# Both halves of the split activations in one 512-column matmul, one PSUM bank per output tile, and modulation pieces on TensorE in pairs

## The chip, the cores and the metric

The kernel runs on one core of a Trainium2 chip. TensorE multiplies, VectorE (DVE) and ScalarE (ACT) do the elementwise work, the queue of SyncE (SP) issues the weight transfers from HBM. The metric is the device time of one execution in microseconds: the median of three runs was 2352.77 us (2349.78 to 2356.88).

## The reference, cut to what matters

Two decoder layers over 256 tokens of width 2048. Each has a mixer and a SwiGLU feed-forward block of inner width 5632, each followed by a residual, a layer norm, and a modulation by vectors computed from the conditioning vector `c`:

```
for layer in range(2):
    mod = silu(c) @ w_ada[layer] + b_ada[layer]              # 6 vectors of 2048
    sh1, sc1, g1, sh2, sc2, g2 = split(mod, 6)
    h = x * (1 + sc1) + sh1
    y = even_mixer(h) if layer == 0 else odd_mixer(h)        # attention + S5 | sliding-window attention
    x = layer_norm(ALPHA * x + g1 * y)
    h = x * (1 + sc2) + sh2
    y = (silu(h @ w_gate) * (h @ w_up)) @ w_down
    x = layer_norm(ALPHA * x + g2 * y)
```

All is float32. Batch is one, so every weight is read from HBM once, for 256 tokens.

## The kernel before

**Layout and arithmetic.** Activations lie transposed: 128 features on the partitions, the 256 tokens along the free dimension, 16 such tiles for a width of 2048. TensorE takes float32r operands. To keep float32 accuracy every operand is split into a high part and the remainder. A weight tile becomes `wh` (a cast on ACT, L262) and `wl` (a subtraction on DVE, L263); an activation tile becomes `hh` and `hl` (in other stages `ah`/`al`, `oh`/`ol`, `ch`/`cl`, `fah`/`fal`). A product of a 128x128 weight tile and a 128x256 activation tile is three matmuls into the same 256 columns of PSUM, wh·hi, wh·lo and wl·hi (L1236 to L1238). This text calls the three a trio. High parts and low parts lie in separate tiles of SBUF.

**Units, pieces, groups.** The weights come as pieces of 512 KB (128x1024): eight weight tiles, one unit. The units are read in the order that `_plan` writes out: phases, each a list of groups, each a list of (k, output tile) pairs. `_k_outer` takes all output tiles of the group for one k before the next k, `_o_outer` finishes one output tile before the next. The phases that matter here: `k2`, `v`, `q`, `glu`, `o0` (mixer of layer 0, about 163 to 516 us), `g00`, `d00`, `g01`, `d01` (its feed-forward block, in two halves of the inner width, to 1286 us), `c1`, `cv`, `c2`, `o1` (mixer of layer 1, to 1566 us), and `g10` to `d11`. A g phase computes gate and up tiles for 22 inner tiles f, a d phase multiplies these by w_down for 16 output tiles.

Pieces wait in a ring of six (`RING`); a piece's slot is given back when its split is done, and then SP issues the next piece. The split tiles `wh`/`wl` have three buffers (`NSPLIT`), so the split of a unit waits until TensorE has done with the unit three before it.

**Modes and PSUM.** Four banks of PSUM (512 float32 columns each) hold sums of the stream, four others serve everything else. In mode B two output tiles share a bank, each in 256 columns. In mode A (phases `v`, `cv`) activations are the stationary operand and 512 columns of weights the moving one (L1259). When a group is done, `evac_group` empties its banks: in a g phase silu on ACT (L1193), product on DVE (L1194), cast on ACT (L1196), remainder on DVE (L1197). In `o0`, `o1` and the d phases `evac_slot` adds a finished tile into the residual z with one DVE instruction (`z_evac`, L924), followed by the statistics of the layer norm.

**Modulation pieces.** Between the weights lie pieces of `w_ada`. Most are multiplied by `c` and summed on DVE (`ada_rows`, L535). Those of five blocks in layer 0 go to TensorE (`ada_block`, L557, `ADA_PE`): a piece holds two k tiles of 512 columns, each multiplied by a stationary operand of 32 columns, in a quarter of the array (`tile_position`); four k tiles in a row use the four quarters. Eight pieces make a block, 40 pieces in all.

**What sets the order.** Code is emitted in the order of the stream loop at the end of `build`. A scheduler then orders each engine's instructions by a simulated time line, keeping the order of instructions that carry the same stamp (`c.front`: splits, loads, sums of modulation pieces). Each engine executes its list strictly in that order.

Of the kernel before, what the change touches and what calls it, by code (L numbers as in the profile page):

```python
# [17 lines left out]
T = 256  # L18
# [38 lines left out]
def _plan():  # L57
    """Phases after the first one: lists of groups (kind, array, tiles of (k, out column tile))."""
# [6 lines left out]
    ph.append(("o0", [("oab", _k_outer(ks, [4 * g + i for i in range(4)])) for g in range(3)]  # L65
               + [("oab", _o_outer(ks, [12, 13, 14, 15]))]))
    for layer in range(2):
        gu, dn = f"gu{layer}", f"dn{layer}"
        if layer == 1:
            ph.append(("c1", [("c", _k_outer(ks, [16, 17, 0, 1, 2, 3, 4, 5]))]))  # L70
            ph.append(("cv", [("c", _k_outer(ks, [18, 19]))]))
            ph.append(("c2", [("c", _k_outer(ks, [6, 7, 8, 9])), ("c", _k_outer(ks, [10, 11, 12, 13])),
                              ("c", _k_outer(ks, [14, 15]))]))
            ph.append(("o1", [("oc", _k_outer(ks, list(range(8)))), ("oc", _k_outer(ks, [8, 9, 10, 11])),
                              ("oc", _o_outer(ks, [12, 13, 14, 15]))]))
        for half in range(2):
            f0 = 22 * half
            sizes = [4] + [2] * 9 if half == 0 else [2] * 11
# [12 lines left out]
def _ada_plan(ph):  # L91
    """Where the pieces of each modulation vector are read: phases -> list of (layer, vector)."""
# [12 lines left out]
def _ada_pieces(l, v):  # L105
    """Pieces of a modulation vector: (l, v, out tile, half of k), or (l, v, block of 4 out tiles, pair of k tiles, 1)."""
# [3 lines left out]
    pcs = [p for _, _, p in sorted([((i + 0.5) / len(a), 0, p) for i, p in enumerate(a)]  # L110
# [20 lines left out]
class Group:  # L131
    def __init__(self, ctx, phase, gi, tiles, mode, nslots, wide=False):
# [9 lines left out]
        self.wide = wide  # L142
# [9 lines left out]
class Ctx:  # L152
# [114 lines left out]
def build(tc, I, out):  # L267
# [3 lines left out]
    with ExitStack() as es:  # L271
        c = Ctx(tc, I, out, es)

# [96 lines left out]
        def s5_params():  # L370
# [51 lines left out]
            # q = (lambda_bar - 1) / lambda  # L422
# [35 lines left out]
            # chunk tables of the rotation  # L458
# [11 lines left out]
            # powers of the output matrices  # L470
# [13 lines left out]
            # powers of the input matrices, turned to stationary operands  # L484
# [37 lines left out]
        accs = {}  # L522

        def ada_front(info, t):
            if len(info) == 4:
                ada_rows(info, t)
            else:
                ada_block(info, t)
# [14 lines left out]
        def ada_block(info, t):  # L543
# [15 lines left out]
            if kg == 7:  # L559
# [27 lines left out]
        hh = [c.slot(0, F32R, "hh"), c.slot(1, F32R, "hh")]  # L587
        hl = [c.slot(2, F32R, "hl"), c.slot(3, F32R, "hl")]

        def hsel(pair, t):  # L590
            return pair[t // 8][:, 256 * (t % 8):256 * (t % 8) + 256]
# [32 lines left out]
        for k in range(KT):  # L624
# [16 lines left out]
            A.copy(hsel(hh, k), xt)  # L641
            V.tensor_sub(hsel(hl, k), xt, hsel(hh, k).bitcast(F32))
            h_hi, h_lo = hsel(hh, k), hsel(hl, k)
            for hf in range(2):
# [3 lines left out]
                for i in range(n_st // 2):  # L648
# [4 lines left out]
                    PE.matmul(o, lhsT=wh[:, W], rhs=h_hi, start=(k == 0 and s % 2 == 0), stop=False, skip_group_check=True)  # L653
                    PE.matmul(o, lhsT=wh[:, W], rhs=h_lo, start=False, stop=False, skip_group_check=True)  # L654
                    PE.matmul(o, lhsT=wl[:, W], rhs=h_hi, start=False, stop=(k == KT - 1), skip_group_check=True)
# [36 lines left out]
        def s5_run(hf):  # L692
# [64 lines left out]
            if hf:  # L757
                S["sh"], S["sl"] = c.slot(9, F32R, "sh"), c.slot(8, F32R, "sl")

            def parts(q):  # L760
                W = slice(512 * q, 512 * q + 512)
                A.copy(S["sh"][:, W], S["s"][:, W])
                V.tensor_sub(S["sl"][:, W], S["s"][:, W], S["sh"][:, W].bitcast(F32))
# [97 lines left out]
        def fox(hd):  # L861
# [39 lines left out]
            W = slice(256 * hd, 256 * hd + 256)  # L901
            A.copy(S["ah"][:, W], op[:, 0:256])
            V.tensor_sub(S["al"][:, W], op[:, 0:256], S["ah"][:, W].bitcast(F32))
            c.aux_put(i3)

# [100 lines left out]
        def ln_tile(L, t, hi, lo):  # L1006
# [600 lines left out]
```

## Time and profile before

| | |
|---|---|
| median of three runs | 2352.77 us |
| profiled execution, first to last instruction | 2353.8 us (the page gives no other time of it) |
| TensorE matmul busy | 2294.5 us, 97% |
| TensorE weight load busy | 2181.5 us, 93% |
| VectorE busy | 1633.4 us, 69% |
| ScalarE busy | 1089.5 us, 46% |
| DMA | 581.66 MB, 247 GB/s on average |
| mean granted TensorE clock | 0.988 |

The profile marks a matmul as busy from its start until its last result is written. Neighbouring matmuls overlap in that, so a busy share near 100% doesn't say how fast they follow each other. That is read from the distances between their starts, in the timeline, or from the number of matmuls in a window.

### The profile page before, as it was taken

The numbers are of one execution on the slowest core, as the hardware profiler recorded it, in microseconds if no ns is written. First come the engines' busy times: TensorE is split into PE (matmuls) and PEld (weight loads), VectorE is DVE, ScalarE is ACT, GpSimd is POOL, SyncE is SP. The second block draws the span as 40 slices with busy tenths as digits, with TensorE's granted clock in tenths as the row PEclk, the third lists the DMA queues.
The fourth block names the chain that finished last, engine by engine and source line by source line (L and its number), as shares of the span: only waits on it lengthen the run. The fifth ranks groups of instructions, "written<-read, shape, count | busy, mean of one in ns | idle before, by whom it ended". The sixth has DMA issues, their size and how long they took to land.

```text
span 2353.8 us, 46216 instructions
## 1 busy us (share of the span) xinstructions
PE 2294.5 (97%) x18990; PEld 2181.5 (93%) x18990; DVE 1633.4 (69%) x2818; ACT 1089.5 (46%) x1657; POOL 5.1 (0%) x11
## 2 busy tenths in 40 slices
PE   7999999999999999999999999999999999999997
PEld 5787787789999999999999988999999999999996
DVE  7638866878777777777786988787666444444466
ACT  3455464356444333444444765565443333444344
POOL 0000000000000000000000000000000000000000
PEclk8999999999999999999999999999999999999998
DMA  8998767858988899898875766357777665666652
GB/s 316 339 324 305 260 223 287 301 186 275 310 311 312 309 302 316 312 311 309 309 254 161 259 232 208 117 154 251 261 266 240 182 186 181 184 183 183 185 181 97
DMA packets 161123, 581.66 MB, mean 247 GB/s; under 512 B 18080, under 2 KB 18608, under 8 KB 160528
## 3 DMA queue, kind: packets, MB, share of 16 engines
q1 hardware_dynamic: 159984, 575.49, 72.9%
q8 instruction: 148, 2.42, 0.4%
q10 hardware_dynamic: 720, 2.66, 0.3%
q0 software_dynamic: 208, 0.57, 0.1%
q14 instruction: 63, 0.52, 0.1%
HBM read 576.55 MB, written 2.10 MB: 246 GB/s over the span
## 4 chain that ended last, share of the span: by engine, by line
PE 92%; DVE 3%; DMA 2%; ACT 2%; issue 1%; ACTq 0%; SPq 0%; DVEq 0%; POOLq 0%
PE acc L1236 27%; PE acc L1238 27%; PE acc L1237 27%; PE acc L1259 1%; PE aux L557 1%; PE ab L630 1%; DMA w<-in_ada_s 1%; DMA w<-in_w_ab 1%; DVE wl L263 1%; ACT wh L262 1%; PE aux L1091 0%; PE aux L787 0%; PE aux L1118 0%; ACT u L703 0%; PE acc L654 0%
## 5 line engine op out<-in xcount | busy, mean ns | idle before, releaser
L263 DVE TENSOR_TENSOR wl<-w,wh 128x1024 fp32r<-128x1024 f32 (+1 forms) x712 | 863.0, 1212 | 606.0 <-ACT wh L262 603.1
L262 ACT CAST wh<-w 128x1024 fp32r<-128x1024 f32 (+1 forms) x712 | 738.7, 1038 | 1025.1 <-PE acc L1237 785.1
L1236 PE MATMUL acc<-hh,wh 128*128 128x256 f32 x3296 | 932.1, 286 | 14.8 <-ACT hh L1017 13.2
L1237 PE MATMUL acc<-hl,wh 128*128 128x256 f32 x3296 | 932.6, 285 | 0.0
L1238 PE MATMUL acc<-hh,wl 128*128 128x256 f32 x3296 | 919.4, 285 | 0.8 <-DVE wl L263 0.8
L1236 PEld LDWEIGHTS acc<-hh,wh 128*128 128x128 f32 x3296 | 634.6, 193 | 25.5 <-ACT hh L1017 14.4
L1237 PEld LDWEIGHTS acc<-hl,wh 128*128 128x128 f32 x3296 | 636.2, 193 | 1.2 <-issue 1.0
L1238 PEld LDWEIGHTS acc<-hh,wl 128*128 128x128 f32 x3296 | 628.0, 193 | 6.5 <-issue 4.5
L1237 PE MATMUL acc<-fal,wh 128*128 128x256 f32 x1408 | 398.3, 283 | 0.0
L1236 PE MATMUL acc<-fah,wh 128*128 128x256 f32 x1408 | 398.1, 283 | 0.0
L1238 PE MATMUL acc<-fah,wl 128*128 128x256 f32 x1408 | 397.5, 283 | 0.0
L535 DVE CUSTOM_DVE_ANT_0 w<-w,crow 128x1024 f32<-128x1024 f32 x280 | 340.9, 1219 | 1.1 <-DMA w<-in_ada 1.0
L1236 PEld LDWEIGHTS acc<-fah,wh 128*128 128x128 f32 x1408 | 270.3, 192 | 0.0
L1237 PEld LDWEIGHTS acc<-fal,wh 128*128 128x128 f32 x1408 | 270.3, 192 | 0.0
L1238 PEld LDWEIGHTS acc<-fah,wl 128*128 128x128 f32 x1408 | 269.7, 192 | 0.1
L1236 PE MATMUL acc<-ch,wh 128*128 128x256 f32 x256 | 73.8, 290 | 0.0
L1238 PE MATMUL acc<-ch,wl 128*128 128x256 f32 x256 | 73.3, 288 | 0.4 <-DVE wl L263 0.4
L1237 PE MATMUL acc<-cl,wh 128*128 128x256 f32 x256 | 73.6, 288 | 0.0
L1193 ACT ACTIVATE ftmp<-acc 128x256 f32<-128x256 f32 x88 | 33.5, 383 | 49.3 <-PE acc L1238 49.3
L924 DVE SCALAR_TENSOR_TENSOR z<-acc,mod,z 128x256 f32<-128x256 f32 x96 | 41.1, 478 | 14.3 <-PE acc L1238 14.3
L1237 PEld LDWEIGHTS acc<-cl,wh 128*128 128x128 f32 x256 | 48.9, 191 | 1.9 <-issue 1.8
L1236 PEld LDWEIGHTS acc<-ch,wh 128*128 128x128 f32 x256 | 48.8, 191 | 1.5 <-issue 1.3
(335 smaller groups left out, 2270.0 us busy)
## 6 DMA issues: line engine op xcount, KB each, us to landing
w<-in_w_gu SPq DMA_DIRECT2D x352, 512.0 KB, 4.5
w<-in_ada SPq DMA_DIRECT2D x320, 512.0 KB, 4.6
w<-in_w_dn SPq DMA_DIRECT2D x176, 512.0 KB, 4.4
w<-in_ada_s SPq DMA_DIRECT2D x64, 512.0 KB, 6.1
w<-in_w_ab SPq DMA_DIRECT2D x40, 512.0 KB, 5.1
w<-in_w_c SPq DMA_DIRECT2D x40, 512.0 KB, 4.3
w<-in_w_oab SPq DMA_DIRECT2D x32, 512.0 KB, 5.5
w<-in_w_oc SPq DMA_DIRECT2D x32, 512.0 KB, 4.0
```

Of the source, the lines that this page charges most:

```text
L262: self.front(nc.scalar.copy(wh[:, :n], src), "act")
L263: self.front(nc.vector.tensor_sub(wl[:, :n], src, wh[:, :n].bitcast(F32)))
L535: c.front(V.tensor_tensor_reduce(t, t, crow[:, 1024 * half:1024 * half + 1024], scale=1.0, scalar=0.0, op0=ALU.mult, op1=ALU.add, accum_ou ...
L557: PE.matmul(bank[32 * j:32 * j + 32, :], lhsT=cs[:, k:k + 32], rhs=t[:, 512 * i:512 * i + 512], start=(k < 4), stop=(k >= 12), skip_group_ ...
L630: PE.matmul(abank[32 * j:32 * j + 32, 0:256], lhsT=cs[:, kk:kk + 32], rhs=t[:, 256 * j:256 * j + 256], start=(q == 0), stop=(q == 3), skip ...
L924: ins = V.scalar_tensor_tensor(zt(L, t), ps_, L["g"][:, t:t + 1], zt(L, t), op0=ALU.mult, op1=ALU.add)
L1193: A.activation(sg, b[:, 0:256], AF.Silu)
L1236: PE.matmul(dst, lhsT=wh[:, W], rhs=hi, start=first, stop=False, skip_group_check=True)
L1237: PE.matmul(dst, lhsT=wh[:, W], rhs=lo, start=False, stop=False, skip_group_check=True)
L1238: PE.matmul(dst, lhsT=wl[:, W], rhs=hi, start=False, stop=(g.left[o] == 0), skip_group_check=True)
L1259: PE.matmul(dst, lhsT=act[:, X], rhs=ww[:, c0:c0 + w], start=first, stop=(last and act is lo), skip_group_check=True)
```

## The change

Activation tiles are laid out in pairs: high and low part of one tile side by side, 512 columns (`pair_of`, `hi_of`, `lo_of`, `both_of`). A new mode D is used for all d phases, for `o0` and `o1` behind their first group, and for all groups of a g phase behind its first one, which now have one f each instead of two. In it a trio is two matmuls (`mm2`): wh with 512 columns, hi and lo at once, into a whole bank, and wl with the 256 columns of hi into the bank's right half. An output tile thus has a bank of its own, and whoever empties it adds the two halves. Phases in mode D other than g take their tiles by `_o_outer`. The modulation pieces of TensorE come two at a time.

```diff
-    ph.append(("o0", [("oab", _k_outer(ks, [4 * g + i for i in range(4)])) for g in range(3)]
-               + [("oab", _o_outer(ks, [12, 13, 14, 15]))]))
+    ph.append(("o0", [("oab", _k_outer(ks, [0, 1, 2, 3]))]
+               + [("oab", _o_outer(ks, [4 * g + i for i in range(4)])) for g in range(1, 4)]))
...
-            sizes = [4] + [2] * 9 if half == 0 else [2] * 11
+            sizes = [4] + [1] * 18 if half == 0 else [1] * 22
...
-            gs = [(dn, _k_outer(kk, [4 * g + i for i in range(4)])) for g in range(3)]
-            gs.append((dn, (_o_outer if half else _k_outer)(kk, [12, 13, 14, 15])))
-            ph.append((f"d{layer}{half}", gs))
+            ph.append((f"d{layer}{half}", [(dn, _o_outer(kk, [4 * g + i for i in range(4)])) for g in range(4)]))
...
-            for i in range(2):
-                k = 2 * kg + i
-                j = k % 4
-                PE.matmul(bank[32 * j:32 * j + 32, :], lhsT=cs[:, k:k + 32], rhs=t[:, 512 * i:512 * i + 512], start=(k < 4),
-                          stop=(k >= 12), skip_group_check=True, tile_position=(0, 32 * j))
+            for j in range(4):
+                k = 2 * kg + j
+                PE.matmul(bank[32 * j:32 * j + 32, :], lhsT=cs[:, k:k + 32], rhs=(t, t2)[j // 2][:, 512 * (j % 2):512 * (j % 2) + 512],
+                          start=(kg == 0), stop=(kg == 6), skip_group_check=True, tile_position=(0, 32 * j))
...
+        def both_of(P, t):
+            return P[t // 4][:, 512 * (t % 4):512 * (t % 4) + 512]
...
+        def mm2(bank, wh, wl, P, k, first, last):
+            PE.matmul(bank, lhsT=wh, rhs=both_of(P, k), start=first, stop=False, skip_group_check=True)
+            PE.matmul(bank[:, 256:512], lhsT=wl, rhs=hi_of(P, k), start=False, stop=last, skip_group_check=True)
...
         def z_evac(L, t, ps_, stats=True):
-            ins = V.scalar_tensor_tensor(zt(L, t), ps_, L["g"][:, t:t + 1], zt(L, t), op0=ALU.mult, op1=ALU.add)
-            if t == KT - 1:
-                c.front(ins)
+            for src in ps_:
+                ins = V.scalar_tensor_tensor(zt(L, t), src, L["g"][:, t:t + 1], zt(L, t), op0=ALU.mult, op1=ALU.add)
+                if t == KT - 1:
+                    c.front(ins)
...
+                    if g.mode == "D":
+                        bg_, bu = g.banks[0], g.banks[1]
+                        A.copy(gs, bg_[:, 256:512])
+                        V.tensor_tensor(gs, bg_[:, 0:256], gs, ALU.add)
+                        A.copy(us, bu[:, 256:512])
+                        V.tensor_tensor(us, bu[:, 0:256], us, ALU.add)
+                        A.activation(sg, gs, AF.Silu)
+                        V.tensor_tensor(a, sg, us, ALU.mult)
```

On TensorE, at the turn from the first g phase to the first d phase, the rows before are plain trios; a d group has two output tiles in one bank (`acc_8478`), one trio of each, then two in the next bank:

```order
L1236 MATMUL acc_8212<-hh_5427,wh_8363 128x256
L1237 MATMUL acc_8212<-hl_5429,wh_8363 128x256
L1238 MATMUL acc_8212<-hh_5427,wl_8364 128x256
L1236 MATMUL acc_8478<-fah_5448,wh_8393 128x256
L1237 MATMUL acc_8478<-fal_5451,wh_8393 128x256
L1238 MATMUL acc_8478<-fah_5448,wl_8394 128x256
L1236 MATMUL acc_8478<-fah_5448,wh_8393 128x256
L1237 MATMUL acc_8478<-fal_5451,wh_8393 128x256
L1238 MATMUL acc_8478<-fah_5448,wl_8394 128x256
L1236 MATMUL acc_8485<-fah_5448,wh_8393 128x256
```

In the changed kernel the trio is the pair L608 and L609. The rows here are those at the end of the fifth unit (`wh_7858`) of that d phase and the start of the sixth (`wh_7884`); `hp_5277` holds the last two activation tiles that the g phase made, `wh_7810` belongs to the third unit:

```order
L608 MATMUL acc_7876<-hp_5276,wh_7858 128x512
L608 MATMUL acc_7816<-hp_5277,wh_7810 128x512
L609 MATMUL acc_7816<-hp_5277,wl_7811 128x256
L609 MATMUL acc_7876<-hp_5276,wl_7859 128x256
L608 MATMUL acc_7876<-hp_5276,wh_7858 128x512
L609 MATMUL acc_7876<-hp_5276,wl_7859 128x256
L608 MATMUL acc_7876<-hp_5276,wh_7884 128x512
L608 MATMUL acc_7947<-hp_5272,wh_7884 128x512
L609 MATMUL acc_7876<-hp_5276,wl_7885 128x256
```

The last trio of the first output tile (`acc_7816`, k = 21) stands two units behind the rest of its unit, and the buffer of the third unit is held until then.

On DVE, in the first g phase, one group of two f stands like this before (`wl` rows are splits, ISA rows are sums of a modulation piece):

```order
L1194 TENSOR_TENSOR ftmp_5447<-ftmp_5447,acc_7132 128x256
L263 TENSOR_TENSOR wl_7390<-w_7293,wh_7389 128x1024
L1194 TENSOR_TENSOR ftmp_5447<-ftmp_5447,acc_7139 128x256
L1197 TENSOR_TENSOR fal_5452<-ftmp_5447,fah_5449 128x256
L263 TENSOR_TENSOR wl_7430<-w_7321,wh_7429 128x1024
L535 ISA w_7327,adap_7319<-w_7327,crow_100 128x1024
L535 ISA adap_7319 128x1
L1197 TENSOR_TENSOR fal_5452<-ftmp_5447,fah_5449 128x256
```

After, a group has one f, and these are its rows:

```order
L1214 TENSOR_TENSOR ftmp_5271<-acc_7490,ftmp_5271 128x256
L262 TENSOR_TENSOR wl_7584<-w_7509,wh_7583 128x1024
L534 ISA w_7515,adap_6889<-w_7515,crow_100 128x1024
L534 ISA adap_6889 128x1
L1216 TENSOR_TENSOR ftmp_5271<-acc_7493,ftmp_5271 128x256
L262 TENSOR_TENSOR wl_7619<-w_7534,wh_7618 128x1024
L534 ISA w_7540,adap_6889<-w_7540,crow_100 128x1024
L534 ISA adap_6889 128x1
L1218 TENSOR_TENSOR ftmp_5271<-ftmp_5271 128x256
L262 TENSOR_TENSOR wl_7644<-w_7559,wh_7643 128x1024
L1225 TENSOR_TENSOR hp_5276<-ftmp_5271,hp_5276 128x256
```

Four evacuation instructions for two f became four for one f, with splits and sums between them.

On TensorE the two halves of a pair of modulation pieces stand next to each other in some places (here in `o0`):

```order
L609 MATMUL acc_4814<-hp_4149,wl_4779 128x256
L556 MATMUL aux_4562<-w_4748,cs_97 32x512 x2
L556 MATMUL aux_4562<-w_4754,cs_97 32x512 x2
L609 MATMUL acc_4882<-hp_3406,wl_4804 128x256
L608 MATMUL acc_4882<-hp_3406,wh_4803 128x512
```

In others (here in `v`) matmuls of the stream stand between them:

```order
L556 MATMUL aux_1851<-w_2231,cs_97 32x512 x2
L1291 MATMUL acc_2235<-wl_2288,hp_122 128x512
L1291 MATMUL acc_2237<-wl_2288,hp_122 128x512
L1291 MATMUL acc_2235<-wh_2287,hp_122 128x512
L1291 MATMUL acc_2237<-wh_2287,hp_122 128x512
L1291 MATMUL acc_2243<-wl_2288,hp_122 128x512
L1291 MATMUL acc_2245<-wl_2288,hp_122 128x512
L1291 MATMUL acc_2243<-wh_2287,hp_122 128x512
L1291 MATMUL acc_2245<-wh_2287,hp_122 128x512
L556 MATMUL aux_1851<-w_2258,cs_97 32x512 x2
```

Of the 20 pairs nine stand like the first and eleven like the second.

## Rows read from the trace of the kernel before

**Rows 1.** The page's head: span, then busy time of each engine
```profile
span 2353.8 us, 46216 instructions
...
PE 2294.5 (97%) x18990; PEld 2181.5 (93%) x18990; DVE 1633.4 (69%) x2818; ACT 1089.5 (46%) x1657; POOL 5.1 (0%) x11
```

**Rows 2.** Busy time by stretch: from:to, length, engines, clock, DMA share, GB/s
```profile
60.00:160.00 100.00, 95.80 (x1011) 77.14 (x1012) 50.05 (x90) 46.14 (x79) 0.31 (x1) 0.99 0.95 336
600.00:1200.00 600.00, 600.00 (x5001) 599.94 (x5000) 458.81 (x635) 242.56 (x286) 0.00 (x0) 1.00 0.89 310
...
400.00:420.00 20.00, 18.02 (x122) 13.51 (x121) 14.50 (x34) 10.15 (x24) 0.00 (x0) 1.00 0.76 261
420.00:440.00 20.00, 20.00 (x153) 17.09 (x152) 15.24 (x30) 6.87 (x7) 0.00 (x0) 1.00 0.84 284
516.00:530.00 14.00, 9.60 (x62) 9.31 (x61) 12.72 (x32) 9.84 (x19) 0.00 (x0) 0.76 0.15 49
1900.00:2000.00 100.00, 100.00 (x836) 100.00 (x835) 47.63 (x48) 37.64 (x40) 0.00 (x0) 1.00 0.60 184
```

**Rows 3.** TensorE's waits, longest first: us in total, times, longest
```profile
PE acc L1236 <- ACT hh L1017: 13.2, 3, 4.4
...
PE acc L1236 <- DVE ftmp L1194: 1.2, 2, 0.9
```

**Rows 4.** Timeline of TensorE in the last g phase: start, length, instruction
```profile
2199.75 0.28 PE L1238 MATMUL acc<-hh,wl 128*128 128x256 f32 x1
...
2202.87 0.28 PE L1237 MATMUL acc<-hl,wh 128*128 128x256 f32 x1
```

**Rows 5.** Timeline of TensorE in phase v, matmuls of 512 columns
```profile
208.40 0.61 PE L1259 MATMUL acc<-wl,hh 128*128 128x512 f32 x2
...
212.03 0.39 PE L1259 MATMUL acc<-wh,hh 128*128 128x512 f32 x1
```

**Rows 6.** Groups of TensorE's instructions by line and shape
```profile
L1236 PE MATMUL acc<-fah,wh 128*128 128x256 f32 x1408 | 398.1, 283 | 0.0
L557 PE MATMUL aux<-w,cs 128*32 128x512 f32 x160 | 41.9, 604 | 3.2 <-DMA w<-in_ada 3.2
```

**Rows 7.** Timeline of TensorE round one modulation piece, and in the first phase
```profile
461.83 1.05 PE L557 MATMUL aux<-w,cs 128*32 128x512 f32 x4
462.81 0.38 PE L1236 MATMUL acc<-oh,wh 128*128 128x256 f32 x1
...
124.70 1.50 PE L630 MATMUL ab<-w,cs 128*32 128x256 f32 x24
126.02 0.28 PE L515 MATMUL kc<-gcr,ebd 128*32 128x64 f32 x2
```

**Rows 8.** Groups of VectorE's and ScalarE's instructions by line and shape
```profile
L263 DVE TENSOR_TENSOR wl<-w,wh 128x1024 fp32r<-128x1024 f32 x680 | 832.4, 1224 | 569.7 <-ACT wh L262 566.9
L535 DVE CUSTOM_DVE_ANT_0 w<-w,crow 128x1024 f32<-128x1024 f32 x280 | 340.9, 1219 | 1.1 <-DMA w<-in_ada 1.0
L924 DVE SCALAR_TENSOR_TENSOR z<-acc,mod,z 128x256 f32<-128x256 f32 x96 | 41.1, 478 | 14.3 <-PE acc L1238 14.3
L1194 DVE TENSOR_TENSOR ftmp<-ftmp,acc 128x256 f32<-128x256 f32 x88 | 36.3, 417 | 8.7 <-ACT ftmp L1193 8.7
...
L262 ACT CAST wh<-w 128x1024 fp32r<-128x1024 f32 x680 | 712.1, 1047 | 991.1 <-PE acc L1237 785.1 <-issue 129.0 <-DMA w<-in_w_ab 24.4
L1196 ACT CAST fah<-ftmp 128x256 fp32r<-128x256 f32 x88 | 35.1, 400 | 1.2 <-DVE ftmp L1194 1.2
L1193 ACT ACTIVATE ftmp<-acc 128x256 f32<-128x256 f32 x88 | 33.5, 383 | 49.3 <-PE acc L1238 49.3
```

**Rows 9.** DMA issues from 600 to 1200 us: count, KB, median us to landing
```profile
w<-in_w_gu SPq DMA_DIRECT2D x144, 512.0 KB, 4.7
w<-in_ada SPq DMA_DIRECT2D x144, 512.0 KB, 4.5
w<-in_w_dn SPq DMA_DIRECT2D x64, 512.0 KB, 4.7
```

More of the change, by code (lines that the diff above doesn't have):

```diff
@@ L131, with __init__ @@
 class Group:
-    def __init__(self, ctx, phase, gi, tiles, mode, nslots, wide=False):
+    def __init__(self, ctx, phase, gi, tiles, mode):
         self.ctx, self.phase, self.gi, self.mode = ctx, phase, gi, mode
@@ L584, in ada_block, with pair_of, hi_of, lo_of @@
                 c.later(1, evac)
[L587 to L591, printed above, removed]
+        def pair_of(*slots):
+            return [c.slot(i, F32R, "hp") for i in slots]
+        def hi_of(P, t):
+            return P[t // 4][:, 512 * (t % 4):512 * (t % 4) + 256]
+        def lo_of(P, t):
+            return P[t // 4][:, 512 * (t % 4) + 256:512 * (t % 4) + 512]
+        def both_of(P, t):
+            return P[t // 4][:, 512 * (t % 4):512 * (t % 4) + 512]
+        def wide_of(P, t, n, part):
+            x = P[t // 4][:, 512 * (t % 4):512 * (t % 4) + 512 * n]
+            return x.rearrange("p (k c n) -> p k c n", c=2, n=T)[:, :, part, :]
+        def mm3(dst, wh, wl, P, k, first, last):
+            PE.matmul(dst, lhsT=wh, rhs=hi_of(P, k), start=first, stop=False, skip_group_check=True)
+            PE.matmul(dst, lhsT=wh, rhs=lo_of(P, k), start=False, stop=False, skip_group_check=True)
+            PE.matmul(dst, lhsT=wl, rhs=hi_of(P, k), start=False, stop=last, skip_group_check=True)
+        def mm2(bank, wh, wl, P, k, first, last):
+            PE.matmul(bank, lhsT=wh, rhs=both_of(P, k), start=first, stop=False, skip_group_check=True)
+            PE.matmul(bank[:, 256:512], lhsT=wl, rhs=hi_of(P, k), start=False, stop=last, skip_group_check=True)
+        hp = pair_of(0, 1, 2, 3)
         n_st = len(_start_tiles())
@@ L652, in build @@
                     W = slice(128 * i, 128 * i + 128)
-                    PE.matmul(o, lhsT=wh[:, W], rhs=h_hi, start=(k == 0 and s % 2 == 0), stop=False, skip_group_check=True)
-                    PE.matmul(o, lhsT=wh[:, W], rhs=h_lo, start=False, stop=False, skip_group_check=True)
-                    PE.matmul(o, lhsT=wl[:, W], rhs=h_hi, start=False, stop=(k == KT - 1), skip_group_check=True)
+                    mm3(o, wh[:, W], wl[:, W], hp, k, k == 0 and s % 2 == 0, k == KT - 1)
             if EK[2] <= k < EK[2] + 4:
@@ L1235, in emit_unit @@
                     W = slice(128 * i, 128 * i + 128)
-                    PE.matmul(dst, lhsT=wh[:, W], rhs=hi, start=first, stop=False, skip_group_check=True)
-                    PE.matmul(dst, lhsT=wh[:, W], rhs=lo, start=False, stop=False, skip_group_check=True)
-                    PE.matmul(dst, lhsT=wl[:, W], rhs=hi, start=False, stop=(g.left[o] == 0), skip_group_check=True)
+                    if g.mode == "D":
+                        mm2(b, wh[:, W], wl[:, W], P, kk, first, g.left[o] == 0)
+                    else:
+                        mm3(dst, wh[:, W], wl[:, W], P, kk, first, g.left[o] == 0)
                     if g.left[o] == 0 and (g.phase in ("o0", "o1") or g.phase[0] == "d"):
@@ L1453, in make_items @@
             mode = "A" if name in ("v", "cv") else "B"
-            wide = bool((name in ("o0", "o1") or (name[0] == "d" and name[2] == "1")) and gi == len(groups) - 1)
-            g = Group(c, name, gi, tiles, mode, None, wide)
+            n_o = len({o for _, o in tiles})
+            if name[0] == "d" or (name in ("o0", "o1") and gi > 0) or (name[0] == "g" and name != "glu" and n_o == 2):
+                mode = "D"
+            g = Group(c, name, gi, tiles, mode)
             assert len(tiles) % UNIT == 0
@@ L1466, in make_items @@
         for j, p in enumerate(pcs):
+            j -= len(p) == 5 and p[3] % 2
             ada.setdefault(units[head + int(j * avail / len(pcs))], []).append(p)
```

118 lines of the change are left out of this document (63 added, 55 removed).

## The prediction

> **What bounds the kernel now.** I read the page's head first. The reader is to see that TensorE is busy nearly all of the time and VectorE for about two thirds [rows 1]; but a busy share says nothing of pace, so the question is how far apart matmuls start. The windows say it: from 600 to 1200 us, 5001 matmuls in 600 us, 0.120 us each, no idle time, full clock; from 1900 to 2000 us the same pace, although VectorE there is busy 48% instead of 76% and the DMA moves 184 GB/s instead of 310 [rows 2]. Two stretches with such different loads elsewhere and one pace: TensorE's own pace is the bound from about 240 us on. The list of its waits confirms it: the longest is 13.2 us for the first activation tiles behind the layer norms [rows 3]. Only the first phase is different (336 GB/s, DMA share 0.95) [rows 2], and nothing there changes but the layout.
>
> So the change is worth what it takes from the start-to-start distances of the trios, less what it adds where TensorE has to wait.
>
> **The trio.** With 256 columns matmuls start every 120 ns: 26 starts between the two rows of [rows 4], 3.12 us. With 512 columns, each with its own weight load (as many loads as matmuls [rows 1]), 16 starts lie between 208.40 and 212.03 us [rows 5]: 226.9 ns. Two of 256 cost 240, one of 512 costs 226.9, so a trio falls from 360 to 346.9 ns. About 13 ns of a matmul's distance don't go with its columns, and the change pays them twice per trio instead of three times. How many trios: the d phases have 1408 [rows 6], the g phases 1280 per layer (the first group of four f stays as it is), o0 192, o1 128: 4288. 4288 x 13.1 ns = 56.2 us. The stages in which these trios lie are at the pace of 120 ns, so I take all of it. Bounds: nothing, where another engine takes over (below), and 56.2.
>
> The Trainium skill (TensorE: Matmul & The Clock Gate, "Back-to-back issue gap") speaks against this: it gives N/2.4 + 2.5 ns between starts, 109 ns for 256 columns and 216 for 512, so that only 2.5 ns per trio would be saved. The trace lies above it by the same 11 ns at both lengths (120 and 226.9), and it decides.
>
> **Modulation pieces on TensorE.** One piece takes 0.98 us from its start to that of the next matmul [rows 7], and there are 160/4 = 40 of them [rows 6]. The first phase shows four quarters of the array at work together: 24 records, six sets of four, take 1.32 us, 0.22 us per set of 256 columns, hence 0.44 for 512 [rows 7]; two sets, 0.88, is what the two-quarter piece takes anyway. A pair whose two halves are issued next to each other should thus cost what one piece costs. By the order on TensorE that holds for 9 pairs of 20; in the others matmuls of the full array stand between, and I see no reason why these should get cheaper. 9 x 0.98 = 8.8 us. Bounds: 0 (the second half waits for its own transfer) and 20 x 0.98 = 19.6.
>
> **Evacuation.** A finished tile of a d phase, o0 or o1 takes two additions into z instead of one, 478 ns more on VectorE [rows 8]. TensorE covers that for 7.6 us per tile (22 trios) or 5.6 (16), except at the end of the four mixer or feed-forward blocks, where layer norm waits for the last tile: 4 x 0.478 = +1.9 us. A group in a g phase gets, per f, two copies on ScalarE (about 0.38 us, as L1193) and two additions on VectorE (as L1194, 0.417) [rows 8]; its banks are wanted again one group later, 16 x 2 x 0.347 = 11.1 us, so the banks hold nobody up. What stands behind these instructions in the queues are the splits. A split has two units of cover, 5.55 us, and takes 1.05 + 1.22 us [rows 8]. From 600 to 1200 us there are 208 units and 144 modulation sums [rows 9], 2.88 us and 0.69 sums per unit. VectorE now works 1.224 + 0.69 x 1.219 + 0.21 = 2.28 us of it; after, 2.28 + 0.21 = 2.49 us of 2.775, 90%. That is high, but below the pace. The same for transfers: 310 GB/s become 322; the first phase ran at 336 [rows 2], and a piece lands in 4.5 to 4.7 us where the ring gives it 6/1.69 units, 9.8 us. I put +2 us for this stretch; bounds 0 and, if VectorE fell back to the old 2.88 us, the whole gain of layer 0's feed-forward block, (704 + 1280) x 13.1 ns = 26.0.
>
> **The turn from g to d.** With k outermost the last f was wanted 84 trios, 30 us, into a d phase, now at 21 x 0.347 = 7.3. The order moves that trio back. In the first d phase so far that the third unit's buffer is given back only when 0.47 us of the fifth unit are left; the sixth needs cast and remainder first, 1.05 + 1.22, with two matmuls (0.45) possible in between. 2.27 - 0.92, and hand-overs: +1.5 us. In the other three the trio stands in the fourth unit, early enough: 0. Bounds 0 and 4 x 2.3. Such a stop is too short to bring the clock down: 2 us without a matmul between 400 and 420 us left it at 1.00, while the gap at 516, at the layer norm, goes with 0.76 over 14 us [rows 2].
>
> **o0.** Tiles now finish every two units instead of four at once every eight, so shift, statistics and double additions (sixteen subtractions and more) meet the last modulation sums within some 12 units, where I count about 38 us of VectorE for about 36 us of TensorE. With two units in reserve: +2 us, bounds 0 and 6.
>
> **Sum**, against the profiled execution: 2353.8 - 56.2 - 8.8 + 1.9 + 2 + 1.5 + 2 = 2296 us. Its span is 1 us above the median of the runs shown; my figure for the median is 2295.
>
> **Rivals**, as medians.
> (a) VectorE becomes the bound in layer 0's feed-forward block. For it: 90% on paper, strict order, and additions that wait for ScalarE's copies ahead of splits. Against it: 24% idle today, nearly all spent waiting for casts (567 us [rows 8]). The 26.0 us are lost instead of the 2: 2319. The Trainium skill says so in general (TensorEngine Tiling (Array Packing), "PSUM Bottleneck"): a faster TensorE doesn't speed up the emptying of PSUM, which may become the bound. No row here shows it yet.
> (b) The 13 ns don't go away with the joined matmul: 226.9 belongs to matmuls of 512 columns in a row, and between those of 256 the pair keeps the 240 of its columns. Then only the small terms are left, 2353.8 - 8.8 + 1.9 + 1.5 + 2, a median of 2349: no change. Against it: the matmuls of [rows 5] alternate between banks and load weights each time, as the new trio does. By the formula of the Trainium skill above, 4288 x 2.5 = 10.7 us would be saved, and the median would be 2340.
> (c) All 20 pairs overlap, 19.6 instead of 8.8: 2284.
> (d) Slower. Place: the 80 groups of one f in the g phases. ScalarE's silu waits for VectorE's addition, and the casts of the next units queue behind it; VectorE's splits wait for these casts. If that makes TensorE wait for one remainder, 1.22 us [rows 8], per group, 98 us are added: 2393. It decides from 61 us / 80 = 0.77 us per group on. For it: ScalarE waits for VectorE today already (L1196 behind L1194, 1.2 us), and there are twice as many such hand-overs. Against it: TensorE waits 1.2 us in total for such evacuations [rows 3], and the two units of reserve.
> That the change doesn't do what it says is so for eleven of the twenty pairs, and is in the sum.
>
> **Chances.** Forecast 0.60 (2282 to 2308 by the bounds of its small terms), (a) 0.18, (b) 0.09, (c) 0.06, (d) 0.07. A measurement of this kernel tells 0.3%, 7 us, from no change. Forecast, (a) and (c) lie beyond that, (b) within it, but for the 0.02 that I give to a part of the saving: faster 0.86, same 0.07, slower 0.07. The range reaches over (c) and (a), 2280 to 2325, and leaves out (b), (d) and some of the edges.
>
> **What would show it.** L608 starting 227 ns before L609, and L609 120 ns before the next L608, in the last g phase: a unit of eight trios in 2.78 us. Between 600 and 1200 us the same unit; if it is 2.88 there and 2.78 in layer 1, it is (a), with TensorE waiting for `wl`. Pairs next to each other at 0.98 us, the others at 0.98 per half. A single stop of 1 to 2 us, in the first d phase, behind the sixth unit's cast. If L608 takes 240 ns, (b); if each g group shows a gap, (d). The forecast is wrong if the feed-forward block of layer 1, where nothing competes, gains less than 20 of its 26 us.

## The result and the profile after

The changed kernel took 2311.4 us in the median of four runs (2310.3 to 2311.9), the kernel before 2354.4 (2349.8 to 2356.9) beside it: ratio 0.9824, 95% interval 0.9809 to 0.9838. A second comparison gave 2312.0 against 2349.9, 0.9834 (0.9817 to 0.9851). Faster by 1.8%, in the direction of the forecast and inside the range; but 16 us above the 2295 of the forecast, so that a good quarter of the expected gain did not come.

The page's head, and the costliest groups of TensorE and VectorE (columns as in [rows 1, 6, 8]):

```profile
span 2310.0 us, 38119 instructions
...
PE 2246.4 (97%) x14702; PEld 1943.2 (84%) x14702; DVE 1726.5 (75%) x3062; ACT 1136.9 (49%) x1817; POOL 5.1 (0%) x11
```

```profile
L608 PE MATMUL acc<-hp,wh 128*128 128x512 f32 x4288 | 1492.2, 397 | 3.6 <-DVE z L943 2.4 <-DVE ftmp L1222 1.2
L609 PE MATMUL acc<-hp,wl 128*128 128x256 f32 x4288 | 1172.8, 280 | 0.9 <-DVE wl L262 0.8
L262 DVE TENSOR_TENSOR wl<-w,wh 128x1024 fp32r<-128x1024 f32 x680 | 832.1, 1224 | 383.7 <-ACT wh L261 369.3 <-PE aux L556 3.9
```

4288 trios, as counted (the second g phase of a layer begins with one f as well, so that all of its groups are in mode D), and hardly an idle microsecond in front of them: 3.6 for L608, 0.9 for L609. The busy time in these rows does not say how far apart matmuls start. The windows do (same columns as [rows 2]):

```profile
600.00:1200.00 600.00, 599.50 (x3426) 522.37 (x3426) 512.35 (x775) 272.60 (x373) 0.00 (x0) 1.00 0.90 315
1900.00:2000.00 100.00, 100.00 (x571) 87.06 (x571) 56.09 (x67) 45.18 (x63) 0.00 (x0) 1.00 0.64 189
```

Against [rows 2] TensorE does more in the same time: 3426 matmuls are 1713 trios in 600 us where 5001 were 1667. That is 350 ns per trio instead of 360, and not the 346.9 of the forecast. Layer 1 (571 in 100 us, 350 ns) has the same pace, with VectorE at 56% instead of 85%. So what is missing is missing in both, in TensorE's own pace, and there is no wait to show for it. The waits that did change are small:

```profile
PE acc L608 <- DVE z L943: 2.4, 1, 2.4
...
PE aux L998 <- DVE z L943: 0.9, 4, 0.2
...
PE acc L609 <- DVE wl L262: 0.8, 3, 0.3
```

The first stands in o1, where its second group wants a bank of its own for each tile while the first group, of eight tiles, is still being emptied (TensorE stands there until an addition into z at 1503 us); the second is the double addition in front of the four layer norms; of the third, two of three lie in the second d phase of layer 0 (1176 and 1179 us).

The missing part is seen in the timeline. These are starts of L608 in the last d phase, with nothing but L609 between them. Both matmuls of a trio write into the same bank, and the next output tile, 22 trios on, takes the next of four banks (start, length, instruction):

```profile
2175.11 0.40 PE L608 MATMUL acc<-hp,wh 128*128 128x512 f32 x1
...
2179.27 0.40 PE L608 MATMUL acc<-hp,wh 128*128 128x512 f32 x1
2179.62 0.62 PE L608 MATMUL acc<-hp,wh 128*128 128x512 f32 x2
...
2182.43 0.40 PE L608 MATMUL acc<-hp,wh 128*128 128x512 f32 x1
...
2199.39 0.40 PE L608 MATMUL acc<-hp,wh 128*128 128x512 f32 x1
```

From the first row to the second are 12 trios in 4.16 us, 346.7 ns each: the forecast. From the fourth to the last 48 trios in 16.96 us, 353.3 ns each. Between the two stand a place where two 512s follow each other (x2) and, 1.5 us behind it, one where two 256s do. Read trio by trio, the first stretch goes 350, 343, 350, 343 ns, the second 350, 361, 349, 350, 361, 349. The 3697 trios of this trace that stand in plain alternation have a mean of 350.8 ns. Where six of them follow each other without a break (2893 places), the mean of the six is 348.3 or less in 38% and above 352 in 61%: there are two paces, and hardly anything between them.

### The profile page after: what moved, and what is told of

The parts are those of the page before. It is cut to its first block, busy times and chain, and to the rows that moved or that the text cites. A ratio compares the mean times of both kernels' runs of the same rounds, so it can differ in the third digit from the quotient of the medians.

```text
span 2310.0 us, 38119 instructions
## 1 busy us (share of the span) xinstructions
PE 2246.4 (97%) x14702; PEld 1943.2 (84%) x14702; DVE 1726.5 (75%) x3062; ACT 1136.9 (49%) x1817; POOL 5.1 (0%) x11
## 4 chain that ended last, share of the span: by engine, by line
PE 91%; DVE 4%; DMA 2%; ACT 2%; issue 1%; ACTq 0%; DVEq 0%; POOLq 0%
PE acc L608 43%; PE acc L609 21%; PE acc L603 6%; PE acc L604 5%; PE acc L605 5%; PE acc L1291 1%; PE ab L650 1%; PE aux L556 1%; DVE wl L262 1%; DMA w<-in_ada_s 1%; DVE w L534 1%; ACT wh L261 1%; PE aux L1125 0%; PE aux L1110 0%; PE aux L1137 0%
## 5 line engine op out<-in xcount | busy, mean ns | idle before, releaser
L608 PE MATMUL acc<-hp,wh 128*128 128x512 f32 x4288 | 1492.2, 397 | 3.6 <-DVE z L943 2.4
L609 PE MATMUL acc<-hp,wl 128*128 128x256 f32 x4288 | 1172.8, 280 | 0.9 <-DVE wl L262 0.8
L608 PEld LDWEIGHTS acc<-hp,wh 128*128 128x128 f32 x4288 | 793.8, 188 | 182.2 <-ACT lnb L963 2.7
L609 PEld LDWEIGHTS acc<-hp,wl 128*128 128x128 f32 x4288 | 810.3, 189 | 21.3 <-DVE wl L262 3.3
L603 PE MATMUL acc<-hp,wh 128*128 128x256 f32 x1120 | 311.6, 294 | 18.9 <-ACT hp L1036 13.2
L604 PE MATMUL acc<-hp,wh 128*128 128x256 f32 x1120 | 317.5, 290 | 1.2 <-DVE hp L921 1.2
L605 PE MATMUL acc<-hp,wl 128*128 128x256 f32 x1120 | 305.6, 292 | 0.0
L603 PEld LDWEIGHTS acc<-hp,wh 128*128 128x128 f32 x1120 | 214.0, 197 | 34.7 <-ACT hp L1036 14.4
L604 PEld LDWEIGHTS acc<-hp,wh 128*128 128x128 f32 x1120 | 219.4, 196 | 8.3 <-issue 4.8
L605 PEld LDWEIGHTS acc<-hp,wl 128*128 128x128 f32 x1120 | 211.1, 196 | 9.1 <-issue 5.3
L943 DVE SCALAR_TENSOR_TENSOR z<-acc,mod,z 128x256 f32<-128x256 f32 x180 | 85.8, 481 | 39.3 <-PE acc L609 34.4
L1214 DVE TENSOR_TENSOR ftmp<-acc,ftmp 128x256 f32<-128x256 f32 x80 | 33.8, 423 | 28.3 <-ACT ftmp L1213 28.3
L1291 PE MATMUL acc<-wh,hp 128*128 128x512 f32 (+1 forms) x192 | 48.3, 360 | 0.1
L650 PE MATMUL ab<-w,cs 128*32 128x256 f32 x512 | 39.4, 409 | 5.1 <-DMA w<-in_ada_s 2.8
L1225 DVE TENSOR_TENSOR hp<-ftmp,hp 128x256 fp32r<-128x256 f32 x88 | 36.6, 420 | 0.1
```

The source lines that it names most:

```text
L603: PE.matmul(dst, lhsT=wh, rhs=hi_of(P, k), start=first, stop=False, skip_group_check=True)
L604: PE.matmul(dst, lhsT=wh, rhs=lo_of(P, k), start=False, stop=False, skip_group_check=True)
L605: PE.matmul(dst, lhsT=wl, rhs=hi_of(P, k), start=False, stop=last, skip_group_check=True)
L608: PE.matmul(bank, lhsT=wh, rhs=both_of(P, k), start=first, stop=False, skip_group_check=True)
L609: PE.matmul(bank[:, 256:512], lhsT=wl, rhs=hi_of(P, k), start=False, stop=last, skip_group_check=True)
L650: PE.matmul(abank[32 * j:32 * j + 32, 0:256], lhsT=cs[:, kk:kk + 32], rhs=t[:, 256 * j:256 * j + 256], start=(q == 0), stop=(q == 3), skip ...
```

## Experiments

**TensorE alone.** The first question was whether the 350 ns belong to TensorE or to what runs beside it. A small kernel, which computes nothing of the reference, lets TensorE go through segments of 96 trios on operands that lie still (`W` is wh, `Wl` wl, `P` hi and lo side by side, `Ph` hi). Two of its segments, cut from their loops:

```diff
+                fr(PE.matmul(banks[1][:, 0:0 + 512], **mm(1, 0, 512, W(i), P(i))))  # S2
+                fr(PE.matmul(banks[1][:, 256:256 + 256], **mm(1, 256, 256, Wl(i), Ph(i))))  # S2
...
+                fr(PE.matmul(banks[4][:, 0:0 + 512], **mm(4, 0, 512, W(i), P(i))))  # S8
+                fr(PE.matmul(banks[5][:, 256:256 + 256], **mm(5, 256, 256, Wl(i), Ph(i))))  # S8
```

> Leaves out the whole computation: TensorE alone runs over operands that lie still in SBUF, segment after segment of 96 trios (or of 96 matmuls, pairs, or 48 quadruples), its output the sums of the banks. What is read are the start-to-start distances. In the changed kernel a trio takes 350 us/1000 in the g phases (two banks in turn) and 353 in the d phases (one bank), 234 to 237 ns behind the 512-column matmul and 116 to 118 behind the one of 256. Theory 1, the mixture itself: TensorE alone needs it, so S2 (512 and 256 of the right half, one bank) and S3 (the same, two banks in turn) give 350 to 353 ns, S1 (three of 256) 360, S5 and S6 (512 only) 227 each. Theory 2, other engines or transfers slow TensorE: S2 and S3 give 347, S1 still 360. Theory 3, the same bank twice in a row costs: S2 353, S3 350, S8 (512 and 256 into different banks) 347 or less, S5 above S6. Theory 4, the weights: a load hides behind the streaming of the matmul before it, and behind a matmul of 256 columns (107 ns at 2.4 GHz) it does not fit wholly, so that the one after a 256 starts late: S10 (512 and 256 on the same weights) differs from S2 by 5 ns or more, and S7 (512, 512, 256, 256) from two S3 trios.

The first and last 512 of S2 (L77) and of S8 (L101):

```profile
53.93 0.40 PE L77 MATMUL b<-hp,wh 128*128 128x512 f32 x1
...
87.50 0.40 PE L77 MATMUL b<-hp,wh 128*128 128x512 f32 x1
...
232.66 0.40 PE L101 MATMUL b<-hp,wh 128*128 128x512 f32 x1
...
265.60 0.39 PE L101 MATMUL b<-hp,wh 128*128 128x512 f32 x1
```

95 distances each: 353.4 ns in S2, 346.7 in S8. Three of 256 (S1) took 359.9, 512s alone 226.7 to 226.9 (S5, S6, S9), S3, S4 and S10 353.2 to 353.4. So other engines and transfers are not needed for the loss (theory 2 falls), nor do the weights matter (S10 as S2). Theory 1 had the mixture right, but S8 doesn't fit it; theory 3 had S8 right and S3 wrong (it asked for 350). Theory 4's quadruple, S7, took 348.2. What fitted most of these numbers was a 256 behind a 512 in the same bank.

**The two parts of the change, each alone**, on one chip. The first run takes the pairs out of the changed kernel (one line of its edit is shown), the second puts them into the kernel before.

```diff
-                ada_block(info, *t)
+                ada_block(info, t)
```

> The change without the pairs: one modulation piece at a time on TensorE, as before, and the joined matmul with a bank per tile kept. By the sum: nine pairs that overlapped no longer do, 9 x 0.98 = 8.8 us more than the changed kernel's 2311, so 2320 and 34 us under the kernel before. If the pairs' gain was only a shift (the time comes back as a wait elsewhere): 2311 to 2313. If all twenty pairs were worth something, through transfers too: 2324 to 2331.

> The kernel before with the modulation pieces in pairs, and nothing else of the change. Seven of its twenty pairs stand next to each other in the order on TensorE, the others have matmuls of the full array between: 7 x 0.98 = 6.9 us less than before, 2347.5. If the parts of the change add up, this gain and that of the joined matmul (34 us) make the 43 us of the whole within 3 us. If the pairs gain only where the trios are joined: 2354. If every pair gains its half: 2335.

Without the pairs: 2317.1 us, ratio 0.9859 (0.9845 to 0.9872), against 0.9824 and 0.9834 for the whole, so the pairs are worth 0.25 to 0.35%, 5.9 to 8.2 us (with the intervals as wide as they are, 0.2% more or less). In the traces all pieces together, each stretch of them from its first start to the next other matmul, hold TensorE for 39.1 us alone and 32.5 us in pairs: 6.6 us. The pairs alone, in the kernel before: 2344.9 us, ratio 0.9975 (0.9966 to 0.9984), 5.1 us between the medians, and 5.2 us in the traces (38.3 before, 33.1 with pairs). The parts add up within the intervals: 0.9859 x 0.9975 = 0.9834. Whole pairs next to each other take what one piece takes, as forecast:

```profile
403.83 1.06 PE L556 MATMUL aux<-w,cs 128*32 128x512 f32 x8
404.83 0.70 PE L916 MATMUL aux<-fox,v 128*128 128x256 f32 x2
```

**Eight and eight.** If a 256 behind a 512 of the same bank costs, it should occur seldom:

```diff
-            PE.matmul(bank[:, 256:512], lhsT=wl, rhs=hi_of(P, k), start=False, stop=last, skip_group_check=True)
+            return lambda: PE.matmul(bank[:, 256:512], lhsT=wl, rhs=hi_of(P, k), start=False, stop=last, skip_group_check=True)
...
-                        mm2(b, wh[:, W], wl[:, W], P, kk, first, g.left[o] == 0)
+                        later.append(mm2(b, wh[:, W], wl[:, W], P, kk, first, g.left[o] == 0))
...
+                for fn in later:
+                    fn()
```

> The changed kernel with one edit: in each unit of eight trios the eight 512-column matmuls come first and the eight of 256 behind them, so that a 256 stands behind a 512 once per unit instead of eight times (some 540 such places in the order instead of 4280). Theory A, the loss sits where a 256-column matmul follows a 512 into the same bank (measured alone: 354 ns per trio in one bank, 347.3 in two): trios fall from 352.0 to about 347.3 ns, 4288 x 4.7 = 20 us, 2291 where the changed kernel is at 2311, ratio to the kernel before 0.973 to 0.975. Theory B, the loss comes from other engines or transfers beside the matmuls: trios stay at 350 to 353, 2311, ratio 0.982. Theory C, the longer run of 512s hands its banks and casts on later, and waits appear (wh given back about 1 us later per unit): 2300 or more in spite of shorter trios.

2306.3 us, ratio 0.9812 (0.9797 to 0.9827): not told apart from the changed kernel by the interval, and 15 us short of theory A. The trace says why: behind the 256s the first five 512s are followed after 233, 236, 229, 232 and 231 ns (medians of 508 runs of eight), and only then after 227. A trio costs 349.1 ns, whether the bank changes (g) or stays (d). So theory A, the bank, doesn't fit, and no wait had come in its place.

**Pairs brought together, and both edits.**

```diff
-            for j in range(4):
+            for j in (2, 0, 3, 1):
...
-                PE.matmul(bank[32 * j:32 * j + 32, :], lhsT=cs[:, k:k + 32], ...)
+                c.front(PE.matmul(bank[32 * j:32 * j + 32, :], lhsT=cs[:, k:k + 32], ...), "pair")
```

> The changed kernel with one edit: the four matmuls of a pair of modulation pieces are issued with the later piece's first, so that the earlier piece's no longer go ahead alone: 17 pairs of 20 stand next to each other instead of 9. Theory A, each pair brought together saves the 0.98 us that one piece costs: 8 x 0.98 = 7.8 us, 2303.5, ratio 0.979. Theory B, a pair waits for the later transfer and TensorE with it: 2311 or more, with waits at the pairs in the trace. Theory C, a pair next to other matmuls was partly overlapped already: 2307.

> Both edits together: eight 512s before eight 256s in each unit, and the pairs of modulation pieces brought together. If they add up: 2311 - 20 - 8 = 2283, ratio 0.970 to 0.972. If VectorE or the transfers bound layer 0's feed-forward block at that pace (it was busy 86% there at 348 ns per trio): its share of the gain, some 9 us, is lost, 2292, with TensorE waiting for casts between 600 and 1200 us.

2309.0 us, ratio 0.9816 (0.9800 to 0.9831), for the pairs brought together: no difference from the changed kernel that can be told (2 to 4 us less by the ratios, which the intervals don't tell from none). The pieces do shrink, from 32.5 to 26.0 us; some of that comes back elsewhere. Here are the stretches 330 to 345 and 345 to 365 us of the changed kernel, and then of this one:

```profile
330.00:345.00 15.00, 13.27 (x148) 9.37 (x147) 10.54 (x15) 13.49 (x17) 1.81 (x1) 1.00 0.82 254
345.00:365.00 20.00, 20.00 (x133) 15.68 (x133) 14.28 (x41) 11.37 (x25) 0.00 (x0) 1.00 0.89 314
```

```profile
330.00:345.00 15.00, 11.77 (x54) 7.28 (x53) 9.78 (x22) 13.14 (x18) 1.18 (x1) 0.76 0.72 245
345.00:365.00 20.00, 20.00 (x113) 13.96 (x112) 11.07 (x28) 8.31 (x18) 0.00 (x0) 0.84 0.57 211
```

```profile
332.74 1.92 PE L556 MATMUL aux<-w,cs 128*32 128x512 f32 x16 [0.62 <-PE acc L605]
336.10 0.39 PE L603 MATMUL acc<-hp,wh 128*128 128x256 f32 x1 [1.44 <-ACT wh L261]
...
338.02 0.79 PE L892 MATMUL aux<-fr,fl 64*128 64x128 f32 x2 [1.18 <-ACT fr L851]
```

TensorE stands 0.62, 1.44 and 1.18 us within six microseconds, twice the 1.7 us of the changed kernel, and the granted clock is 0.76 and then 0.84 where it was 1.00, part of these stretches at 1.2 GHz instead of 2.4. At those clocks 15 and 20 us hold at most 0.24 x 15 + 0.16 x 20 = 6.8 us less work, about as much as the 6.5 us that the pieces gave; that the one took back the other is an estimate, not shown. Nor is it shown that the stops bring the clock down, for the kernel before was low there too, with 1.1 us of stops:

```profile
330.00:345.00 15.00, 13.90 (x73) 10.84 (x74) 12.14 (x31) 14.17 (x29) 0.00 (x0) 0.77 0.51 176
```

So the changed kernel gained up to 0.23 x 15 = 3.5 us there by the clock alone, which no term of the forecast had. Both edits together took 2302.8 us, ratio 0.9789 (0.9776 to 0.9803): short of the 2283, and of the 2292 too, though TensorE waits for nothing between 600 and 1200 us. The clock is low from 330 to 365 us in this kernel as well (0.86 and 0.77).

**TensorE alone, again.** With the same instructions, other banks and runs of other lengths:

> Leaves out the whole computation, as the first measurement of TensorE alone: 96 trios (a 512-column matmul and one of 256 into the right half) per segment, every matmul with a weight load of its own. Known so far: 354.0 ns per trio with both in one bank, 347.3 with the 512 always in one bank and the 256 always in another, 360 for three of 256, 226.9 for 512 after 512; and in the kernel with eight 512s ahead of eight 256s 349.1, where the first five 512s behind the 256s start 229 to 235 ns apart instead of 227. Theory A, a 256 behind a 512 in the same bank is what costs: T1, T2 and T5 354, T3 347; T4 (512 A, 256 B, 512 B, 256 A) 347; runs in one bank fall as one over their length, 7.1 / n above 346.9: T6 350.4, T7 348.7, T8 347.8, T9 347.1; T11 (runs of eight, the 256s in another bank) 346.9. Theory B, every change of length costs, in whatever bank, some 18 ns per round trip once the runs are long enough: T8, T10 and T11 349.1 all, T9 347.5, T6 and T7 between 354 and 349. Theory C, the bank itself matters (its number, not the change): T3 in banks 0 and 1 differs from 347.3 in banks 4 and 5, T2 in banks 4 and 5 from 354.0 in banks 2 and 3.

T3, which is S8 but for the numbers of its banks, first and last 512:

```profile
87.25 0.40 PE L80 MATMUL b<-hp,wh 128*128 128x512 f32 x1
...
120.81 0.40 PE L80 MATMUL b<-hp,wh 128*128 128x512 f32 x1
```

33.56 us over 95 distances: 353.3, not 346.7. All of T1 to T5 are at 353.3. Theory A falls by that, and T1 and T2, in banks 4 and 5 as S8 was, speak against theory C. Runs of two gave 348.3 ns, of four 350.6, of eight 349.1 to 349.2, in one bank (T8), two in turn (T10) or with the 256s in another (T11), and of 32 347.4. For the runs of eight that is theory B. Beside its banks, and the chip of the run, what differs between S8 and T3 is what ran before.

> Leaves out the whole computation: TensorE alone. Known: in one segment the alternation of a 512-column matmul and one of 256 went on at 353.3 ns per trio to its end (trios of 350, 361, 349 in turn), in another, with the same instructions but for the bank, at 346.7 (350, 343 in turn); both stand in the changed kernel too, and go over into each other where two 512s and two 256s follow each other. Theory A, two sequences that keep themselves up: which of them runs depends on what went before, not on banks, weights or other engines. Then here, in one bank throughout, both appear: after a 512, 512, 256, 256 (n = 2) the next 23 trios change from 353.3 to 346.7 or back, so that the ten stretches are at one of the two figures and none between, and an extra 512 or 256 between two stretches changes it too or never does. Theory B, the bank decides: all stretches here (bank 4) are at 353.3, whatever stands between. Theory C, it drifts: stretches change in their middle, without an event. The fourteen unit patterns behind them (eight trios each, runs of n 512s ahead of n 256s) then have one figure each between 346.7 and 353.3 that does not hang on the state before, if their runs set the state anew: runs of eight 349.2, of two 348.3, as measured before; a pattern under 348 would be worth putting in the kernel, (351.5 - 347.5) x 4288 = 17 us.

One bank, stretches of 23 trios, with two 512s and two 256s between them (x2):

```profile
18.90 0.39 PE L71 MATMUL b<-hp,wh 128*128 128x512 f32 x1
...
27.01 0.64 PE L71 MATMUL b<-hp,wh 128*128 128x512 f32 x2
27.72 0.40 PE L71 MATMUL b<-hp,wh 128*128 128x512 f32 x1
...
35.70 0.62 PE L71 MATMUL b<-hp,wh 128*128 128x512 f32 x2
36.39 0.40 PE L71 MATMUL b<-hp,wh 128*128 128x512 f32 x1
...
44.52 0.62 PE L71 MATMUL b<-hp,wh 128*128 128x512 f32 x2
```

8.11 us, then 7.98, then 8.13 for 23 trios: 353, 347, 353 ns. Same instructions, same bank, no other engine at work: two sequences that keep themselves up, and the doubled place turns one into the other. It does not always: the third one, at 44.52 us, found the slow sequence and left it slow. Runs of three, four and eight left the slow one as it was (seven of seven); of four extra 512s the first left it slow, the second turned it fast and the other two left it fast, as all four extra 256s did. No stretch changed in its middle. Theory A holds in its core; what it said of the doubled place and the extra matmuls was too simple, perhaps because it matters which point of the sequence they meet; that wasn't tested. Of the fourteen unit patterns one lay under 348: six 512s, six 256s, two and two, 347.5 ns in every unit from the second on.

**The order that does not hang on the state**, in the kernel (with `mm2` as in eight and eight), with and without the pairs brought together, and the changed kernel itself on the same chip:

```diff
-                        mm2(b, wh[:, W], wl[:, W], P, kk, first, g.left[o] == 0)
+                        second.append(mm2(b, wh[:, W], wl[:, W], P, kk, first, g.left[o] == 0))
+                        if i in (5, 7):
+                            for fn in second:
+                                fn()
+                            second = []
```

> The changed kernel as it is, timed beside the two that follow on the same chip: 2311 within 4 us, ratio 0.981 to 0.984. Its trios go on at 346.7 or 353.3 ns by what stood before them, 352.0 on average with what lies between.

> The changed kernel with the trios of each unit of eight in the order 512 x6, 256 x6, 512 x2, 256 x2, which TensorE alone ran at 347.5 ns per trio in every unit, whatever stood before (singles ran at 346.7 or 353.3, eight and eight at 349.2). Theory A, the state of TensorE's own sequence is what the changed kernel loses: 4288 x (352.0 - 347.5) = 19 us less by the distances; 1 ns per trio of this average lies in waits that stay, so 14 to 17 us: 2296, ratio 0.975 to 0.977. Theory B, in the kernel the weight loads and transfers disturb it, and a fixed order gives no more than eight and eight did (3 to 5 us): 2307. Theory C, the later release of banks and buffers makes waits: over 2307.

> The same order of trios, and the pairs of modulation pieces brought together (17 of 20 instead of 9). With the changed kernel's trios that edit took 6.5 us off the pieces and gave back 5 in a stop at 333 us, after which the granted clock stood at 0.76 and 0.84 for some 30 us. If the stop is there again: 2295, 1 us less than the run before; if it is gone: 2289, ratio 0.972 to 0.974.

2312.0 us for the changed kernel (0.9834), 2299.1 (2298.1 to 2303.6) with the order of six and two, ratio 0.9782 (0.9766 to 0.9798), and 2295.3 (2293.9 to 2298.9) with the pairs as well, 0.9765 (0.9749 to 0.9780). The order is worth 13 us, a little under theory A's 14 to 17. Its windows and its timeline in the last d phase:

```profile
600.00:1200.00 600.00, 600.00 (x3454) 528.05 (x3453) 509.17 (x783) 278.17 (x376) 0.00 (x0) 1.00 0.90 316
1900.00:2000.00 100.00, 100.00 (x578) 88.00 (x577) 55.62 (x70) 45.97 (x64) 0.00 (x0) 1.00 0.65 189
```

```profile
2181.48 1.53 PE L608 MATMUL acc<-hp,wh 128*128 128x512 f32 x6
...
2184.26 1.53 PE L608 MATMUL acc<-hp,wh 128*128 128x512 f32 x6
```

A unit of eight trios now takes 2.78 us, 347.5 ns each, the same as TensorE alone, and 3454 matmuls fit where 3426 did. In the last kernel the stop at 330 us and the low clock behind it are there again:

```profile
330.00:345.00 15.00, 11.77 (x128) 8.29 (x126) 9.95 (x17) 12.71 (x19) 1.80 (x1) 0.87 0.82 272
345.00:365.00 20.00, 20.00 (x104) 13.97 (x103) 11.65 (x35) 9.36 (x21) 0.00 (x0) 0.76 0.56 207
```

So the 3.8 us between the last two, whose intervals overlap, are all that the pairs brought together gave; a version without that stop wasn't tried. It is the fastest kernel of this study.

## Why the prediction was right, and where it was not

**The range: right in part by luck.** The 2311.4 lie above the band that the forecast had for itself, 2282 to 2308. The range reaches to 2325 to take in rival (a), and (a) is not what happened.

**What bounds the kernel: right.** TensorE's pace set the time before and after. Both the stretch with busy VectorE and DMA and the one without run at 350 ns.

**The trio: the term that was mis-sized.** The step was "Two of 256 cost 240, one of 512 costs 226.9, so a trio falls from 360 to 346.9 ns", and "I take all of it". I took the 226.9 of 512s among 512s [rows 5] and the 120 of 256s among 256s [rows 4] and added them for an alternation that no row of before showed. In it the sum holds in some stretches (346.7) and not in others (353.3). The mean, 350.8, makes 4288 x 9.2 = 39.4 us instead of 56.2. These 16.8 us are the bulk of the miss; the pieces below add 3.0, and small terms that did not come take some 4 away. The cause is shown on TensorE alone, in one bank, and in the kernel by an order that avoids it and gains 13 us. Even where the sum holds, its parts do not: in the stretches of 346.7 L609 follows some 232 ns behind L608 and the next L608 some 115 behind L609, not 227 and 120. Why the total comes out all the same no run here shows. My own sign for a wrong forecast, less than 20 of 26 us in layer 1's feed-forward block, came true: its four phases take 746.2 us instead of 764.2, a gain of 18.0.

**Rival (b)** had the right suspicion, that a joined matmul among 256s may not keep the distance of [rows 5], with the wrong price: of the 13.1 ns 6.4 go in the stretches of 353.3 and 3.9 on average, not all. Its sign (L608 at 240 ns) is met in part: L609 follows 234.9 ns behind L608 on average, but in the stretches of 353.3 every third one follows after 240 to 242.

**Modulation pieces: right in the mechanism, smaller in size.** 8.8 forecast; 5.8 less TensorE time in the traces (38.3 before, now 32.5) and 5.9 to 8.2 in the comparison. Seven stretches of eight matmuls, 1.0 to 1.2 us each, take 7.2 us for 14 pieces of 0.98, 6.5 less. The other two of the nine pairs stand in one stretch of sixteen, 2.1 us, and brought nothing, because in the kernel before four pieces stood together already, 1.85 us to the next matmul, which the forecast's 40 pieces of 0.98 overlooked:

```profile
344.96 1.92 PE L557 MATMUL aux<-w,cs 128*32 128x512 f32 x16
346.81 0.39 PE L1238 MATMUL acc<-hh,wl 128*128 128x256 f32 x1
```

Two pieces that other matmuls cut in two halves, 0.98 each, cost 2.0 more (before, one piece was cut so). Rival (c), all twenty: with 17 together another 6.5 us of pieces went, but the time fell by only 2 to 4, within the noise.

**Small terms.** Double additions at the layer norms: 0.9 us in four waits, forecast 1.9. Layer 0's VectorE: forecast +2, measured 0, since its feed-forward block gained the same 18.0 as layer 1's; between 600 and 1200 us it is busy 85% (I had 90%, having added up 2.28 us per unit before where [rows 2] give 458.81 / 208 = 2.21, and for units that follow faster than they do), and TensorE waits for no remainder between 520 and 1170 us. Rival (a) is false, since layer 0 and layer 1 have one pace. The stop in the first d phase: forecast +1.5, none is there. Not foreseen: 2.4 us in o1, for its banks; with that the mixer of layer 1, from layer norm to layer norm, takes 276.8 us instead of 275.0, so that there the change costs more than its 128 trios bring. What o0's crowding cost can't be separated: from its first matmul to the first of the next phase it takes 118.1 us instead of 118.9, with 192 x 9.2 = 1.8 us less in trios, and TensorE stands idle for 7.8 us of it instead of 6.4. Rival (d) is false: TensorE never waits for the sums of the groups of one f. The 1.2 us in the row of L608 above are for the product (L1222) of the first group of four f, which stayed as it was, with the same 1.2 us as before [rows 3]. In its price the 61 us should be 58 (2353 - 2295); and with 10.7 us saved (b) comes to 2339, not 2340. Nothing hangs on either.

**The sum again**, with what was measured: 2353.8 - 39.4 - 5.8 + 2.4 + 0.9 = 2311.9, against a span of 2310.0. That they agree within 2 us proves no single term: the sum takes the mean of plain alternation for all 4288 trios, and leaves out the clock at 330 us, up to 3.5 us, and other small waits.

## What to carry to other kernels

A distance between starts holds for the row of matmuls in which it was read; where a change mixes lengths, measure the mixture, or give a range that reaches half way back to the old pace. When a gain is missing and no wait shows it, read the starts one by one: a mean of 350 was 346.7 in some stretches and 353.3 in others. And where work is taken out of a stretch with stops, look at the granted clock of that stretch in both traces: 6.5 us of work saved there bought 2 to 4, within the noise, in a stretch whose clock was lower than in the changed kernel.

## What the runs showed of the hardware

On TensorE alternating matmuls of 512 and 256 columns, each with its own weight load, go on in one of two ways: trios of 350, 361, 349 ns in turn (mean 353.3), or of 350 and 343, sometimes 346 and 347 (mean 346.7 to 347.1). In one bank, with no other engine at work, both occur, and what stood before decides; each lasted as long as nothing broke the alternation. After a run of 256s the first 512s start up to 236 ns apart before they come to 227, and behind eight 512s the first 256 is followed after 113 or 114 ns instead of 120 (T8, T10 and T11, in 35 of 36 places). What inside TensorE makes this is open: no run here shows it.
